# Turning the second FFN's gated tiles by VectorE in 32x32 blocks and by transfers between partition groups

## The chip, the core and the metric

The kernel runs on one core of a Trainium2 chip. TensorE multiplies matrices, VectorE and ScalarE do elementwise work, GpSimd issues the accumulating transfers and SyncE the plain ones; 16 DMA engines carry both. The metric is the device time of one execution in microseconds (us), the median of three runs, 2597.21.

## The reference, cut to what matters

One transformer-like layer: a half-step FFN, token mixing, a second half-step FFN, and a final norm. What the change touches is the second FFN:

```
def half_step_ffn(x, mod, i, g, w_up, w_down):
    h = adaln(x, g, mod, i)
    a, b = jnp.split(h @ w_up, 2, axis=-1)
    return x + 0.5 * mod[:, i + 2, None, :] * ((jax.nn.silu(a) * b) @ w_down)
```

Here x has 256 tokens of 2048 features, and the hidden width is 5632. The gated tensor silu(a) * b comes out with tokens on the partitions, and the product with w_down wants hidden rows on the partitions: each 128x128 piece must be turned.

## The kernel before

Every fp32 weight tile of 128x2048 (1 MB) comes from HBM, and `split` (L128, L129) makes of each half a rounded part `hi` (ScalarE) and a rest `lo` (VectorE); `mm3` (L152) makes three products of the parts. The pools hold four halves of hi and lo, three plain tiles `raw`, and two pairs of kept tiles, `chain` and `ra`.

The hidden width is cut into eleven blocks of 512. Block 0 and block 10 are computed directly. Blocks 1 to 9 go through `quad(n)`: a product of 2x2 sub-blocks in seven instead of eight products, over two token halves t = 0 and 1. Its seven steps run in the order a11, a12, n1, s4, s2, s3, a22, each over two weight tiles, q = 0 and 1, so over four halves; their results stand in the PSUM tiles X and Y. The tiles `ca` and `cy` gather them into the gated 128x512 tile of each token half: t = 0 is ready after s2 (`c12`), t = 1 after a22 (`c21`). The next block begins with a11.

The weights of a block are sums, made in part by accumulating transfers. SyncE issues: `again` (L2121), the two tiles with which the next block starts; `plain` (L2125), two raw tiles; the two plain loads in `first` (L2130); and `load_split` (L143), the down-projection's raw tiles. GpSimd issues the accumulating ones (`accum`, L731). chain and ra change roles from block to block. Beside the seven steps a unit of the down-projection, `down(n, n + 1)`, runs after four of them (after a12, n1, s2 and s3 of each block): one raw tile, and `mm <- hid2h, hid2l`.

`turned()` (L2041) turns a waiting gated tile N_TURN = 2 steps after it was made: four transposes on TensorE into PSUM (L2055), then the same two parts, hid2h by ScalarE (L2058, with the sign) and hid2l by VectorE (L2060). An order of steps is written by hand in `sequence`; the framework places each engine's instructions by its own plan, and every engine works through its list in order, so an instruction that waits holds all behind it. Each transfer signals on one of eight completion lanes for SyncE (DMAHW0 to 7), taken in turn, and eight for GpSimd (DMASW); a lane is taken again when its last transfer has landed.

## Time and profile before

| | |
|---|---|
| runs | 2602.92, 2593.06, 2597.21 us, median 2597.21 |
| profiled execution, its span | 2595.9 us |
| TensorE busy | 2570.6 us, 99% |
| VectorE, ScalarE, GpSimd busy | 2190.7, 1431.0, 220.6 us |
| granted TensorE clock, mean | 0.997 |
| moved from HBM | 664.59 MB read |
| second FFN's blocks 1 to 8 | about 2008 to 2492 us of the span, 60.6 us each |

How to read it: a row of a timeline has the start and the duration in us, the engine (SPq and POOLq are the issues of SyncE and GpSimd), the line, the operation, what is written and read, and how many. In brackets stands the idle time before and what ended it. In a row of groups, after the bar: busy us, the mean ns of one, then the idle time before. A row of waits has the total in us, how often, and the longest. A transfer's last figure is the time from issue to landing in us. Block 4's cycle begins near 2190 us.

### The profile page before, as it was taken

Reading aid. Unit: us, or ns where it says so; the run is one execution under the profiler, and the core shown is the slowest. Engines: PE = TensorE matmul, PEld = TensorE weight load, DVE = VectorE, ACT = ScalarE, POOL = GpSimd, SP = SyncE. Lnnn points to the kernel's source line nnn. Section 1 sums busy time; section 2 is a strip of 40 time slices with the busy share of each in tenths; the row PEclk is TensorE's granted clock in tenths of the full one; section 3 lists DMA queues with packets and bytes.
Section 4 is the critical chain, followed back from the end, with each engine's and each line's share of the span. In section 5 each row is a group of like instructions: output and inputs, shape, how many; then the busy total and the mean of one; then the engine's idle time right before and its main releaser. Section 6 shows DMA issues by size and latency. Waiting matters only on the chain. (4 is left out here: it accounts for less than half of the span.)

```text
span 2595.9 us, 34150 instructions
## 1 busy us (share of the span) xinstructions
PE 2570.6 (99%) x12646; PEld 2138.6 (82%) x12646; DVE 2190.7 (84%) x2884; ACT 1431.0 (55%) x1838; POOL 220.6 (8%) x271
## 2 busy tenths in 40 slices
PE   8999999999999999999999999999999999999998
PEld 5688888888888888888889989888898888888887
DVE  7788888878888788888887898798889888888887
ACT  5354444545444465444454448456486676666664
POOL 0000000100001100000110000120000000001001
PEclk9999999999999999999999999999999999999999
DMA  9889999999999989989986897776768999999985
GB/s 399 340 220 264 265 291 266 263 275 288 260 291 253 280 249 243 214 223 225 225 257 256 294 326 241 239 278 218 260 235 250 275 274 284 278 281 279 272 247 173
DMA packets 127655, 684.71 MB, mean 264 GB/s; under 512 B 14200, under 2 KB 16760, under 8 KB 64896
## 3 DMA queue, kind: packets, MB, share of 16 engines
q1 hardware_dynamic: 98112, 490.63, 50.4%
q0 software_dynamic: 29376, 191.90, 37.5%
q8 instruction: 99, 1.62, 0.2%
q14 instruction: 68, 0.56, 0.1%
HBM read 664.59 MB, written 17.89 MB: 263 GB/s over the span
## 5 line engine op out<-in xcount | busy, mean ns | idle before, releaser
L128 ACT ACTIVATE hi<-raw 128x1024 fp32r<-128x1024 f32 (+2 forms) x488 | 505.6, 1040 | 411.4 <-PE mm L152 314.0
L129 DVE TENSOR_TENSOR lo<-raw,hi 128x1024 fp32r<-128x1024 f32 (+2 forms) x476 | 569.3, 1204 | 137.9 <-ACT hi L128 117.7
L128 ACT ACTIVATE hi<-chain 128x1024 fp32r<-128x1024 f32 x352 | 372.0, 1060 | 305.0 <-PE mm L152 174.2
L129 DVE TENSOR_TENSOR lo<-chain,hi 128x1024 fp32r<-128x1024 f32 x352 | 426.5, 1221 | 106.9 <-ACT hi L128 98.1
L152 PE MATMUL mm<-hi,hhi 128*128 128x512 f32 (+3 forms) x1024 | 394.2, 385 | 0.0
L152 PE MATMUL mm<-lo,hhi 128*128 128x512 f32 (+3 forms) x1024 | 387.0, 378 | 0.2 <-DVE lo L129 0.2
L152 PE MATMUL mm<-hi,hlo 128*128 128x512 f32 (+3 forms) x1024 | 386.4, 377 | 0.0
L208 DVE SCALAR_TENSOR_TENSOR junk<-sraw,cBh 128x1024 fp8e5<-128x1024 f32 x192 | 234.4, 1221 | 22.8 <-DMA sraw<-in_w_mt 20.5
L152 PEld LDWEIGHTS mm<-lo,hhi 128*128 128x128 f32 x1024 | 192.5, 188 | 34.5 <-DVE lo L129 0.6
L152 PEld LDWEIGHTS mm<-hi,hhi 128*128 128x128 f32 x1024 | 192.6, 188 | 31.3 <-ACT hi L128 0.4
L152 PEld LDWEIGHTS mm<-hi,hlo 128*128 128x128 f32 x1024 | 192.8, 188 | 30.7
L129 DVE TENSOR_TENSOR lo<-ra,hi 128x1024 fp32r<-128x1024 f32 x104 | 126.3, 1222 | 27.2 <-ACT hi L128 23.1
L128 ACT ACTIVATE hi<-ra 128x1024 fp32r<-128x1024 f32 x104 | 110.1, 1061 | 67.6 <-PE mm L152 40.8
L152 PE MATMUL mm<-hi,hid2h 128*128 128x512 f32 x352 | 137.0, 389 | 0.0
L152 PE MATMUL mm<-lo,hid2h 128*128 128x512 f32 x352 | 137.0, 389 | 0.0
L152 PE MATMUL mm<-hi,hid2l 128*128 128x512 f32 x352 | 137.0, 389 | 0.0
L152 PE MATMUL mm<-hi,sumshl 128*128 128x512 f32 x400 | 123.1, 389 | 0.0
L731 POOL DMA_DIRECT2D chain<-in_w_up1b x60 | 53.0, 884 | 731.2 <-DVE lo L129 731.2
L208 DVE SCALAR_TENSOR_TENSOR sr<-sr,cBl 128x1024 f32<-128x1024 f32 x84 | 102.0, 1222 | 15.2 <-DMA sr<-in_w_mt 14.5
L152 PE MATMUL mm<-hi,sumshh 128*128 128x512 f32 x352 | 108.3, 389 | 0.0
L152 PE MATMUL mm<-hhi,hi 128*128 128x512 f32 (+1 forms) x288 | 101.4, 352 | 0.0
L152 PE MATMUL mm<-hhi,lo 128*128 128x512 f32 (+1 forms) x288 | 99.0, 344 | 0.0
(490 smaller groups left out, 5451.0 us busy)
## 6 DMA issues: line engine op xcount, KB each, us to landing
raw<-in_w_dn SPq DMA_DIRECT2D x70, 1024.0 KB, 9.3
chain<-in_w_up1b POOLq DMA_DIRECT2D x60, 1024.0 KB, 10.8
sraw<-in_w_mt SPq DMA_DIRECT2D x96, 512.0 KB, 8.4
sr<-in_w_mt SPq DMA_DIRECT2D x81, 512.0 KB, 5.4
raw<-in_w_up1b SPq DMA_DIRECT2D x40, 1024.0 KB, 8.0
mraw<-in_w_m SPq DMA_DIRECT2D x32, 1024.0 KB, 7.5
chain<-in_w_dn POOLq DMA_DIRECT2D x30, 1024.0 KB, 8.9
chain<-in_w_up2b POOLq DMA_DIRECT2D x28, 1024.0 KB, 11.1
```

What stands on the lines that cost most here:

```text
L128: scalar[0].activation(hi, src, AF.Copy)
L129: vector[0].tensor_tensor(lo, src, hi.bitcast(F32), op=ALU.subtract)
L152: tensor[0].matmul(out_ap, s, m, start=first and not n, stop=last and n == 2, skip_group_check=skip)
L208: ins = nc.vector.scalar_tensor_tensor(junk() if junk else raw, raw, 1.0, cB[s], op0=ALU.mult, op1=ALU.mult, accum_out=mT[:, i, s, kt, h : ...
L731: accum = lambda dst, src: nc.gpsimd.dma_start(dst, src, accum_op=ALU.add)
```

## The change

The gated tiles of blocks 1 to 8 no longer pass through TensorE. VectorE turns each 32x32 block of a 128x512 tile in place of its own (`nc.vector.transpose`, into the spare tile that held the other factor: ca for t = 0, cy for t = 1). A step later SyncE issues 16 transfers from SBUF to SBUF, each of 32 partitions x 128 elements (16 KB), which move partition group a of the spare tile to group b of a new tile x, of which there is one. Four steps after the turn hid2h and hid2l are made from x, with an output in runs of 32. The sign now goes into the gated product. The hidden rows stand in another order in a block, so the host lays out w_ffn2_down's rows for these blocks accordingly, in tiles of the same size. Block 9 and block 10 keep TensorE's transposes; N_TURN falls from 2 to 1.

```
-N_TURN = 2
+N_TURN = 1
+N_MOVE = 4
...
-            n, t, sa, sign = turn[0]
+            n, t, sa, spare = turn[0]
...
-            tb = tbank()
-            for j in range(FB):
-                nc.tensor.transpose(tb[:, j * P : (j + 1) * P], sa[:, j * P : (j + 1) * P], ident)
-            t3 = tb.rearrange("p (j c) -> p j c", j=FB)
             hh, hl = (x[:, :, t * P : (t + 1) * P] for x in hids[n])
-            nc.scalar.activation(hh, t3, AF.Copy, scale=sign)
-            if sign < 0:
-                nc.vector.scalar_tensor_tensor(hl, t3, -1.0, hh.bitcast(F32), op0=ALU.mult, op1=ALU.subtract)
-            else:
-                nc.vector.tensor_tensor(hl, t3, hh.bitcast(F32), op=ALU.subtract)
-            done.add((n, t))
+            if spare is None:
+                tb = tbank()
...
+                return
+            nc.vector.transpose(spare, sa)
+            x = f2b.tile([P, CB], F32, name="x", bufs=1)
+            by_runs = lambda y: y.rearrange("p j (a c) -> p a j c", c=32)
+            moved.append((clock[0], x, spare, n, t, by_runs(hh), by_runs(hl), x.rearrange("p (a j c) -> p a j c", a=4, j=FB)))
+
+        def parts_of(hh, hl, x):
+            nc.scalar.activation(hh, x, AF.Copy)
+            nc.vector.tensor_tensor(hl, x, hh.bitcast(F32), op=ALU.subtract)
+
+        def arrived():
+            for then, x, spare, n, t, *parts in list(moved):
+                if clock[0] == then + 1:
+                    for a in range(4):
+                        for b in range(4):
+                            dst, src = (slice(32 * i, 32 * i + 32) for i in (b, a))
+                            nc.sync.dma_start(x[dst, a * P : (a + 1) * P], spare[src, b * P : (b + 1) * P])
+                elif clock[0] == then + N_MOVE:
+                    parts_of(*parts)
+                    done.add((n, t))
+                    moved.pop(0)
...
-            mul = lambda o, x, y: nc.vector.tensor_tensor(o, x, y, op=ALU.mult)
+            negative = lambda o, y: nc.vector.scalar_tensor_tensor(o, o, -1.0, y, op0=ALU.mult, op1=ALU.mult)
...
-                mul(g["a"], g["a"], g["b"])
-                wait_turn(n, 0, g["a"], -1.0)
+                negative(g["a"], g["b"])
+                wait_turn(n, 0, g["a"], g["b"] if n != QUADS[-1] else None)
...
-                mul(g["a"], g["a"], g["y"])
-                wait_turn(n, 1, g["a"], -1.0)
+                negative(g["a"], g["y"])
+                wait_turn(n, 1, g["a"], g["y"] if n != QUADS[-1] else None)
```

The order on SyncE in block 4, before: the two raw tiles of `plain`, the two chain tiles of `again`, a down-projection tile, the two ra tiles of `first`, three down-projection tiles.

```order
L2125 DMA raw<-in_w_up2b 128x2048 x2
L2121 DMA chain_16106<-in_w_up2b 128x2048
L2121 DMA chain_16107<-in_w_up2b 128x2048
L143 DMA raw<-in_w_dn 128x2048
L2130 DMA ra_16108<-in_w_up2b 128x2048
L2130 DMA ra_16109<-in_w_up2b 128x2048
L143 DMA raw<-in_w_dn 128x2048 x3
```

The same stretch of SyncE's list now:

```order
L2149 DMA raw<-in_w_up2b 128x2048 x2
L2145 DMA chain_16106<-in_w_up2b 128x2048
L2083 DMA x<-ca 32x128 x16
L2145 DMA chain_16107<-in_w_up2b 128x2048
L2154 DMA ra_16108<-in_w_up2b 128x2048
L2154 DMA ra_16109<-in_w_up2b 128x2048
L145 DMA raw<-in_w_dn 128x2048
L2083 DMA x<-cy 32x128 x16
L145 DMA raw<-in_w_dn 128x2048 x3
```

All 16 pieces of t = 0 stand between the two chain tiles, the first down-projection tile has moved behind the ra tiles, and t = 1's 16 pieces stand behind it. Blocks 1, 2, 6 and 8 have t = 0's pieces in this place too; in 3, 5 and 7 four of them stand ahead of the second tile of `again`, and twelve behind it.

The same place with SyncE's waits, from the first chain tile to the ninth piece (a transfer's own lane is the first DMAHW that it waits for, where there is one; the first piece also waits for VectorE's turn):

```order
L2145 DMA chain_16106<-in_w_up2b 128x2048 [waits DMAHW6_49,DMASW2_49,DVE_49]
L2083 DMA x<-ca 32x128 [waits DMAHW1_49,DMAHW7_49,DMAHW0_49,DVE_49]
L2083 DMA x<-ca 32x128 x3
L2083 DMA x<-ca 32x128 [waits DMAHW3_49]
L2083 DMA x<-ca 32x128 [waits DMAHW4_49]
L2083 DMA x<-ca 32x128 [waits DMAHW5_49]
L2083 DMA x<-ca 32x128 [waits DMAHW6_49]
L2083 DMA x<-ca 32x128 [waits DMAHW7_49]
```

The first chain tile is on lane 6, the pieces take lanes 7, 0, 1, 2 and so on, and the eighth waits for lane 6, which is that chain tile's landing.

On ScalarE, around the last tile of a22 in block 4, before (L2105 is the copy of X in `c22`, L2109 the silu in `c21`):

```order
L2058 ACTIVATE hid2h<-tr 128x4x128
L128 ACTIVATE hi<-raw 128x1024 x2
L128 ACTIVATE hi<-ra_16108 128x1024 x2
L2105 ACTIVATE ca<-X 128x512
L128 ACTIVATE hi<-ra_16109 128x1024 x2
L128 ACTIVATE hi<-chain_16106 128x1024 x2
```

And now:

```order
L2129 ACTIVATE ca<-X 128x512
L130 ACTIVATE hi<-ra_16109 128x1024
L2071 ACTIVATE hid2h<-x 128x4x4x32
L130 ACTIVATE hi<-ra_16109 128x1024
L130 ACTIVATE hi<-chain_16106 128x1024 x2
```

The hid2h copy of t = 0 has moved from ahead of the down-projection's halves to between the two halves of a22's last tile, and it waits for all eight lanes on which its pieces land.

More of the change, by code (lines that the diff above doesn't have):

```diff
@@ L2052, in turned, with wait_turn @@
             turn.pop(0)
-            tb = tbank()
-            for j in range(FB):
-                nc.tensor.transpose(tb[:, j * P : (j + 1) * P], sa[:, j * P : (j + 1) * P], ident)
-            t3 = tb.rearrange("p (j c) -> p j c", j=FB)
             hh, hl = (x[:, :, t * P : (t + 1) * P] for x in hids[n])
-            nc.scalar.activation(hh, t3, AF.Copy, scale=sign)
-            if sign < 0:
-                nc.vector.scalar_tensor_tensor(hl, t3, -1.0, hh.bitcast(F32), op0=ALU.mult, op1=ALU.subtract)
-            else:
-                nc.vector.tensor_tensor(hl, t3, hh.bitcast(F32), op=ALU.subtract)
-            done.add((n, t))
+            if spare is None:
+                tb = tbank()
+                for j in range(FB):
+                    nc.tensor.transpose(tb[:, j * P : (j + 1) * P], sa[:, j * P : (j + 1) * P], ident)
+                x = tb.rearrange("p (j c) -> p j c", j=FB)
+                parts_of(hh, hl, x)
+                done.add((n, t))
[7 more added lines that the diff above has]
+            nc.vector.tensor_tensor(hl, x, hh.bitcast(F32), op=ALU.subtract)
+        moved = []
+        def arrived():
[7 more added lines that the diff above has]
+                    parts_of(*parts)
+                    done.add((n, t))
+                    moved.pop(0)
         done = set()
-        def wait_turn(n, t, sa, sign):
-            turn.append((n, t, sa, sign))
+        def wait_turn(n, t, sa, spare):
+            turn.append((n, t, sa, spare))
             born[n, t] = clock[0]
@@ L2193, in up @@
                                 nc.vector.tensor_tensor(sab[t], sab[t], bs[t], op=ALU.mult)
-                                wait_turn(n, t, sab[t], 1.0)
+                                wait_turn(n, t, sab[t], None)
                             else:
@@ L2265, in tile_layer @@
             clock[0] += 1
+            arrived()
             turned()
@@ L2268, in tile_layer @@
             assert next(x, x) is x
-        while turn:
+        while turn or moved:
             clock[0] += 1
+            arrived()
             turned()
@@ L2376, in _laid_out @@
     m["w_mt"] = asc(wm[:, 2:].reshape(D, 7, KT, P).transpose(1, 2, 3, 0))
+    runs = lambda dn: dn.reshape(NF // FB, 4, FB, 32, NCB, CB).transpose(0, 4, 1, 3, 2, 5).reshape(NF // FB, NCB, P, 2048)
     for n in "12":
@@ L2391, in _laid_out @@
         m[f"w_pre{n}"] = asc(np.concatenate(loads))
-        m[f"w_dn{n}"] = asc(dn.reshape(NF // FB, FB, P, NCB, CB).transpose(0, 3, 2, 1, 4).reshape(NF // FB, NCB, P, 2048))
+        rows = dn.reshape(NF // FB, FB, P, NCB, CB).transpose(0, 3, 2, 1, 4).reshape(NF // FB, NCB, P, 2048)
+        if n == "2":
+            rows = np.concatenate([rows[:1], runs(dn)[1:-2], rows[-2:]])
+        m[f"w_dn{n}"] = asc(rows)
     w = a["w_in"][0]
```

## The prediction

> **What bounds the kernel now.** I read the page first, then the table of stretches for the second FFN, SyncE's waits, SyncE's issues of one block, and last TensorE, ScalarE and the transfers around those issues.

> ```profile
> span 2595.9 us, 34150 instructions
> PE 2570.6 (99%) x12646; PEld 2138.6 (82%) x12646; DVE 2190.7 (84%) x2884; ACT 1431.0 (55%) x1838; POOL 220.6 (8%) x271
> 2189.40:2250.00 60.60, 60.20 (x270) 49.39 (x269) 53.52 (x52) 41.06 (x44) 4.91 (x6) 1.00 0.93 273
> ```

> The first two rows are the page's: TensorE is busy for 99% of the span. The third is one stretch of 60.6 us, the length of one block of the second FFN, with the busy time of PE, PEld, DVE, ACT and POOL, the granted clock, the DMA engines' share and GB/s. TensorE lacks 0.4 us there, VectorE works 53.5 us, and the 16 DMA engines are taken for 93%. So TensorE sets the end, and DMA comes close behind it. What is in reserve shows in stretches of 2 us inside this block:

> ```profile
> 2204.00:2206.00 2.00, 2.00 (x10) 1.68 (x9) 1.31 (x2) 0.13 (x1) 0.00 (x0) 1.00 1.02 422
> 2210.00:2212.00 2.00, 2.00 (x11) 1.65 (x10) 2.00 (x3) 1.61 (x2) 0.00 (x0) 1.00 1.03 434
> 2232.00:2234.00 2.00, 2.00 (x11) 1.64 (x9) 1.97 (x3) 2.00 (x4) 0.00 (x0) 1.00 0.46 193
> 2234.00:2236.00 2.00, 1.59 (x7) 1.03 (x6) 2.00 (x3) 1.07 (x2) 0.00 (x0) 1.00 0.02 8
> 2236.00:2238.00 2.00, 2.00 (x10) 1.62 (x10) 2.00 (x2) 1.34 (x2) 0.00 (x0) 1.00 0.04 4
> ```

> The DMA share is 1.0 except for about 5 us, 2233 to 2238. That is the whole reserve of a block, and it comes late in the cycle. Next, what SyncE's queue waits for in the same block, and its issues:

> ```profile
> SPq L2125 <- DVE lo L129: 21.5, 2, 14.7
> SPq L143 <- DVE lo L129: 15.2, 4, 7.9
> 2190.22 0.33 SPq L2125 DMA_DIRECT2D raw<-in_w_up2b  x1
> 2193.31 5.39 SPq L2121 DMA_DIRECT2D chain<-in_w_up2b  x2
> 2201.56 0.33 SPq L143 DMA_DIRECT2D raw<-in_w_dn  x1
> 2204.66 5.82 SPq L2130 DMA_DIRECT2D ra<-in_w_up2b  x2
> 2218.41 5.76 SPq L143 DMA_DIRECT2D raw<-in_w_dn  x3
> ```

> SyncE waits most of the time for VectorE to leave a weight buffer, and issues a load the moment it may. The loads are just in time, so whatever holds this queue delays them. I call the two chain loads G1 (2193.3) and G2 (it ends with the row, so 2198.4), the ra loads R1 and R2, the first down-projection load D1 (2201.6). Their landings (KB, us from issue to landing: G1, G2, then D2 at 2218.4, then the raw load at 2237.0, alone on the engines):

> ```profile
> chain<-in_w_up2b SPq DMA_DIRECT2D x1, 1024.0 KB, 13.5
> chain<-in_w_up2b SPq DMA_DIRECT2D x1, 1024.0 KB, 10.9
> raw<-in_w_dn SPq DMA_DIRECT2D x1, 1024.0 KB, 11.8
> raw<-in_w_up2b SPq DMA_DIRECT2D x1, 1024.0 KB, 4.7
> ```

> **What is taken from TensorE.** 16 tiles with four transposes each leave; blocks 9 and 10 keep theirs. One group in block 4:

> ```profile
> 2195.83 0.40 PE L152 MATMUL mm<-lo,hid2h 128*128 128x512 f32 x1
> 2196.07 0.60 PE L2055 MATMUL tr<-ident,ca 128*128 128x128 f32 x4
> 2196.43 0.71 PE L152 MATMUL X<-hi,s3f 128*128 128x512 f32 x2
> 2196.97 0.39 PE L152 MATMUL X<-lo,s3f 128*128 128x512 f32 x1
> ...
> 2197.65 0.39 PE L152 MATMUL X<-lo,s3f 128*128 128x512 f32 x1
> ```

> From one lo product to the next is 0.68 us in steady state (2196.97 to 2197.65), and 1.14 across the group (2195.83 to 2196.97): 0.46 us a group, and 16 x 0.46 = 7.4 us on the path. This is all that the change can give, beside the 0.4 us a block that TensorE idles.

> **The arithmetic around it** moves little:

> ```profile
> L2078 DVE TENSOR_TENSOR ca<-ca 128x512 f32<-128x512 f32 x9 | 6.2, 685 | 0.0
> L2060 DVE SCALAR_TENSOR_TENSOR hid2l<-tr,hid2h 128x512 fp32r<-128x512 f32 x16 | 10.9, 683 | 0.0
> L2077 DVE TENSOR_TENSOR chain<-chain,ra 128x1024 f32<-128x1024 f32 x16 | 19.2, 1220 | 0.1
> L2058 ACT ACTIVATE hid2h<-tr 128x512 fp32r<-128x512 f32 x16 | 9.4, 588 | 0.7 <-PE tr L2055 0.4
> ```

> The gated product becomes a scalar_tensor_tensor and the lo part a tensor_tensor: 683 against 685 ns, nothing. ScalarE's copy keeps 588 ns; source and strides differ, for which I take 0 between -0.1 and +0.2 us a tile, off the path. VectorE gains one 32x32 turn of 128x512: no row shows one, so between 0.69 us (a pass of that size) and 1.22 (twice the elements), and I take 0.7. That is 1.4 us a block on an engine with 7 us free; its cover is that idle time, and if it fails up to 2.4 us a block show.

> **SyncE's queue and the transfers.** This is where I expect the price. Each tile adds 16 transfers of 16 KB, 256 in all, on the queue that feeds the weights. Nearest rows for price and pace: a transfer of exactly 32 rows of 512 bytes (how long it took, then its issue and the next one's), a 256 KB one at the program's end, and a queue that has eight transfers out:

> ```profile
> cc<-in_cc SPq DMA_DIRECT2D x1, 16.0 KB, 1.6
> 0.80 0.40 SPq L190 DMA_DIRECT2D cc<-in_cc  x1
> 1.25 0.41 SPq L601 DMA_DIRECT2D vecs<-in_vecs  x1
> out<-acc SPq DMA_DIRECT2D x1, 256.0 KB, 2.3
> 7.16 0.33 SPq L421 DMA_DIRECT2D raw<-in_w_pre  x1
> SPq L421 <- DMA mraw<-in_w_m: 1.3, 1, 1.3
> ```

> One lands after 1.6 (16 KB) to 2.3 us (256 KB); I take 2.0. An issue costs 0.33 us alone; back to back, 0.80 to 1.25, it is 0.45, whatever the size. I take 0.45; the ends are 0 and 0.6. The last two rows are the ninth transfer of the program, held until the third had landed: SyncE uses eight completion lanes in turn and waits for the lane. The built program has these waits on the new transfers (quoted with the change): in block 4 G1 holds lane 6 and x's eighth piece needs lane 6. So piece 8 cannot go before G1 has landed, and G2, R1, R2, D1 stand behind all 16.

> Of DMA time the pieces are small: 256 KB a tile at the 422 to 434 GB/s above are 0.6 us, and at half that pace 1.2, so 1.2 to 2.4 us a block against a reserve of 5.

> Block 4, step by step. G1 lands at 2193.3 + 13.5 = 2206.8. Piece 8 goes then, pieces 9 to 16 follow at 0.45, the last at 2210.4, landed at 2212.4. G2 goes at 2210.9 and not at 2198.4: the engines, full till G1's end, stand nearly empty for some 5 us.

> Who waits for x? ScalarE: its hid2h copy now stands between two weight copies, and whatever follows waits behind it.

> ```profile
> 2206.06 1.06 ACT L128 ACTIVATE hi<-ra 128x1024 fp32r<-128x1024 f32 x1 [1.93 <-PE mm L152]
> 2207.43 1.06 ACT L128 ACTIVATE hi<-ra 128x1024 fp32r<-128x1024 f32 x1 [0.31 <-PE mm L152]
> 2220.19 1.05 ACT L128 ACTIVATE hi<-raw 128x1024 fp32r<-128x1024 f32 x1
> 2211.48 0.39 PE L152 MATMUL Y<-hi,h2hi 128*128 128x512 f32 x1
> 2224.24 0.39 PE L152 MATMUL mm<-hi,hid2h 128*128 128x512 f32 x1
> ```

> It stands between the first two rows. ScalarE resumes at 2212.4: 0.59 for hid2h, 1.06 for hi, then 1.22 on VectorE for lo, 2215.3. TensorE wants this half at 2211.48 (fourth row: fourth half of the product that begins at 2207.40), less the 0.46 saved: 2211.0. It waits 4.3 us.

> R2 waits for that lo: 2215.4; D1 behind it: 2215.8, 14 us late. Alone it would land 4.7 later and be in time. But the next two accumulating loads are on the engines then, as they were for D2, so I take D2's 11.8: 2227.6, and 2229.9 as hi and lo. TensorE wants it at 2224.24 (fifth row; the third is ScalarE's copy of it), less 0.92 saved, plus 4.3: 2227.6. Another 2.3 us. Together 6.6 us.

> The second tile of a block (cy) queues behind D1 and ahead of D2, D3 and D4. D2's use moves with the 6.6 us, D3 and D4 are wanted far later: nothing, at most 2 us.

> Blocks 1, 2, 6 and 8 have the same order. In 3, 5 and 7 G2 goes after four pieces, in time, but a later piece needs its lane: G2 lands at 2198.4 + 10.9 = 2209.3, the last piece goes at 2211.1, lands at 2213.1. The hid2h copy stands one half into the next product, so the half is ready at 2213.1 + 2.9 = 2216.0, wanted at 2207.40 + 5 x 1.36 (the 2211.48 of the fourth half gives 4.08 for three) - 0.46 = 2213.7: 2.3 us. D1 goes at 2212.4, is ready at 2226.5, wanted at 2225.6: 0.9. Together 3.2.

> Sum: 5 x 6.6 + 3 x 3.2 - 7.4 = 35.2 us. The profiled span of 2595.9 becomes 2631; it lies 1.3 us under the median of 2597.2 of the three runs, so I say **2632 us**. Low end: issues that cost nothing and 1.6 us landings leave 1.9 and 0.1 us, and D1 in time: 9.8 - 7.4 = +2.4, 2600. High end: D1 with G1's 13.5 adds 1.7 us to each block, and 2 us for the second tile: +30, 2662.

> [...]

> **Rivals.** (a) The queue has room and the transfers hide: 2597 - 7, 2590, no change that can be measured. For it: D1 is issued 18.6 us ahead of its copy. Against: G1's 13.5 us are in the trace and the lane makes the queue wait them out. It decides if pieces land by 2208.1: then the half is ready at 2211.0. (b) TensorE's clock drops at the new stalls. The trace knows half clock early on:

> ```profile
> 18.00:28.00 10.00, 9.91 (x57) 5.75 (x59) 7.87 (x19) 8.42 (x16) 1.18 (x2) 0.50 1.02 424
> ```

> Ten us at 0.50, after a start with idle gaps, cost 5 us. One such time in each of the five longer-stalled blocks, plus 25: 2657. For it: 4.3 us without work. Against: no gap in this stage is that long, so nothing shows it. [...] (c) The waits land elsewhere: the second tile holds ScalarE as well, another 3 us a block, 2656. (d) It is faster by more than 0.5%, 13 us: more than the 7.4 + 8 x 0.4 that TensorE can give; only an error of mine.

> **Chances.** Forecast, 2610 to 2650: 0.58. (a), with everything down to a few us of loss: 0.22. (b) and (c): 0.17. (d): 0.03. Half a per cent, 13 us, is about what a measurement of this kernel tells from no change; so slower 0.75, same 0.22, faster 0.03. The range 2600 to 2665 leaves out about 0.12 below and 0.05 above.

> **What the profile after would show.** SyncE's waits gain a large group on x, put down to G1's and G2's landings; G2 goes 10 us later after VectorE's release in five blocks; ScalarE shows idle before hid2h<-x, some 3 to 6 us a tile for ca; TensorE's idle in the blocks rises from 0.4 us to 3 to 7, before a22's last half and before the first down-projection of each block; DMA's share shows a second hole after G1. If the issues of x take no longer than before and ScalarE never idles there, the prediction is wrong, and 2590 is right. If TensorE idles but before n1 or s4, the place is wrong.

## The result, and the profile after

The changed kernel takes 2698.4 us (median of four runs, 2695.64 to 2699.29) against 2598.84: the ratio is 1.0389, 95% interval 1.0377 to 1.0401. The direction was forecast, the size was not: +100 us instead of +35.

The page's first rows after, the span and the busy time of each engine:

```profile
span 2697.6 us, 34416 instructions
PE 2605.2 (97%) x12582; PEld 2149.6 (80%) x12582; DVE 2200.4 (82%) x2900; ACT 1426.5 (53%) x1838; POOL 220.4 (8%) x271
```

TensorE has 64 matmuls less to do and is busy for 34.6 us more (2605.2 against 2570.6). The rest of its span, where it is not busy, has grown from 25.3 to 92.4 us, by 67.1. The two make 101.7 us, the difference of the two profiled spans. So there are two separate losses: TensorE waits, and TensorE runs slower. First the waits, TensorE's in the second FFN (total, how often, longest):

```profile
PE Y L154 <- ACT hi L130: 28.8, 9, 5.3
PE mm L154 <- ACT hi L130: 20.0, 6, 10.2
PE X L154 <- ACT hi L130: 7.9, 3, 3.0
PE mm L154 <- DVE lo L131: 6.0, 8, 2.0
PE Y L154 <- DVE lo L131: 4.7, 8, 1.0
```

It never waits for hid2h; but for 0.2 us it waits for the two parts of a weight half. Y is mostly a22's product, X the next block's a11, mm the down-projection. Who keeps ScalarE, in the same stretch:

```profile
ACT hid2h L2071 <- DMA x<-ca: 49.8, 8, 7.6
ACT hi L130 <- DMA raw<-in_w_dn: 34.9, 12, 6.2
ACT hid2h L2071 <- DMA x<-cy: 25.0, 8, 9.5
```

Two things: its in-order wait for x, for both tiles of a block, and weights that land late. And SyncE's queue on the new transfers:

```profile
SPq L2083 <- DVE cy L2064: 42.2, 6, 7.8
SPq L2083 <- DMA x<-cy: 31.3, 27, 1.8
SPq L2083 <- DMA raw<-in_w_up2b: 29.6, 8, 4.4
SPq L2083 <- DMA raw<-in_w_dn: 21.4, 5, 6.5
SPq L2083 <- DMA ra<-in_w_up2b: 19.8, 4, 6.6
SPq L2083 <- DMA chain<-in_w_up2b: 15.4, 4, 4.3
```

The last four rows, 86 us, are the lane waits: a piece stands until a 1 MB load has landed. The first is the queue standing at a piece whose tile VectorE has not yet turned.

The chain in block 4, as a timeline of SyncE's issues:

```profile
2235.20 0.33 SPq L2145 DMA_DIRECT2D chain<-in_w_up2b  x1
2236.54 18.54 SPq L2083 DMA_DIRECT2D x<-ca  x16
2255.19 0.52 SPq L2145 DMA_DIRECT2D chain<-in_w_up2b  x1
...
2259.67 0.42 SPq L145 DMA_DIRECT2D raw<-in_w_dn  x1
```

And the timeline of ScalarE's copy from x and of TensorE around it (in brackets the idle time before):

```profile
2256.43 0.63 ACT L2071 ACTIVATE hid2h<-x 128x512 fp32r<-128x512 f32 x1 [6.41 <-DMA x<-ca]
...
2252.68 0.39 PE L154 MATMUL Y<-lo,h2hi 128*128 128x512 f32 x1
2258.06 0.79 PE L154 MATMUL Y<-hi,h2hi 128*128 128x512 f32 x1 [4.99 <-ACT hi L130]
2258.65 0.63 PE L154 MATMUL Y<-hi,h2lo 128*128 128x512 f32 x1
...
2275.78 0.50 PE L154 MATMUL mm<-hi,hid2h 128*128 128x512 f32 x1 [2.37 <-ACT hi L130]
```

G1 goes at 2235.2; the 16 pieces hold the queue for 18.5 us; G2 goes 20 us behind G1. ScalarE stands 6.4 us at x, TensorE 5.0 us at a22's last half and 2.4 us at the first down-projection. The forecast was 17.6 us for G2's lag and 4.3 and 2.3 us for TensorE's two stalls. What it left out stands in the fourth row: a product that took 0.39 us ahead of the stall takes 0.63 behind it. The same place as stretches (PE's busy time first, the granted clock third from the end):

```profile
2258.00:2263.60 5.60, 5.50 (x12) 3.91 (x13) 5.57 (x6) 3.94 (x6) 0.87 (x1) 0.50 0.98 407
2263.60:2270.40 6.80, 6.80 (x31) 5.59 (x31) 6.02 (x7) 5.17 (x6) 0.87 (x1) 1.00 1.02 292
```

Half clock for 5.6 us of work behind a stall of 5: 12 matmuls where the next 6.8 us have 31. The clock record of the trace has 15 such stretches between 2024 and 2571 us, 81.9 us in all; before there was none in this stage.

### The profile page after: what moved, and what is told of

It reads as the page before. It is cut to its first block, busy times and chain, and to the rows that moved or that the text cites. A ratio compares the mean times of both kernels' runs of the same rounds, so it can differ in the third digit from the quotient of the medians.

```text
span 2697.6 us, 34416 instructions
## 1 busy us (share of the span) xinstructions
PE 2605.2 (97%) x12582; PEld 2149.6 (80%) x12582; DVE 2200.4 (82%) x2900; ACT 1426.5 (53%) x1838; POOL 220.4 (8%) x271
## 3 DMA queue, kind: packets, MB, share of 16 engines
q8 instruction: 99, 1.62, 0.2%
## 4 chain that ended last, share of the span: by engine, by line
PE 28%; DMA 11%; DVE 5%; SPq 3%; issue 2%; ACT 2%; ACTq 0%; POOL 0%; POOLq 0%; DVEq 0%
PE mm L154 18%; DMA x<-cy 4%; PE Y L154 3%; SPq L2083 3%; PE X L154 2%; DMA ra<-in_w_up2b 2%; DVE lo L131 2%; DMA chain<-in_w_up2b 2%; DMA raw<-in_w_dn 1%; ACT hi L130 1%; DMA sr<-in_w_mt 1%; DMA x<-ca 1%; PE mm L1707 1%; PE tr L154 0%; PE tr L1527 0%
## 5 line engine op out<-in xcount | busy, mean ns | idle before, releaser
L131 DVE TENSOR_TENSOR lo<-chain,hi 128x1024 fp32r<-128x1024 f32 x352 | 425.6, 1220 | 106.0 <-ACT hi L130 100.5
L210 DVE SCALAR_TENSOR_TENSOR junk<-sraw,cBh 128x1024 fp8e5<-128x1024 f32 x192 | 234.2, 1220 | 21.5 <-DMA sraw<-in_w_mt 19.1
L154 PE MATMUL mm<-hi,hid2h 128*128 128x512 f32 x352 | 143.4, 407 | 20.0 <-ACT hi L130 20.0
L131 DVE TENSOR_TENSOR lo<-ra,hi 128x1024 fp32r<-128x1024 f32 x104 | 126.1, 1221 | 31.5 <-ACT hi L130 28.4
## 6 DMA issues: line engine op xcount, KB each, us to landing
raw<-in_w_dn SPq DMA_DIRECT2D x70, 1024.0 KB, 6.8
chain<-in_w_up1b POOLq DMA_DIRECT2D x60, 1024.0 KB, 9.8
raw<-in_w_up1b SPq DMA_DIRECT2D x40, 1024.0 KB, 8.3
mraw<-in_w_m SPq DMA_DIRECT2D x32, 1024.0 KB, 7.4
chain<-in_w_dn POOLq DMA_DIRECT2D x30, 1024.0 KB, 8.3
chain<-in_w_up2b POOLq DMA_DIRECT2D x28, 1024.0 KB, 13.1
```

What stands on the lines that cost most here:

```text
L131: vector[0].tensor_tensor(lo, src, hi.bitcast(F32), op=ALU.subtract)
L154: tensor[0].matmul(out_ap, s, m, start=first and not n, stop=last and n == 2, skip_group_check=skip)
L210: ins = nc.vector.scalar_tensor_tensor(junk() if junk else raw, raw, 1.0, cB[s], op0=ALU.mult, op1=ALU.mult, accum_out=mT[:, i, s, kt, h : ...
```

## The experiments

The theory after the result, Q: the pieces hold SyncE's queue, so weights land late (its half L), and ScalarE waits for x in order (its half S); TensorE's clock falls at the stalls. Its rivals: the time the pieces take on the DMA engines (D), and the new arithmetic (V). One table for all runs; a ratio is to runs of the kernel before that were made beside it, whose medians lie between 2594.73 and 2599.69 us; the two last columns are each profile's "not busy" (span less TensorE's busy time) and busy time, less those of the kernel before (25.3 and 2570.6 us).

| run | median, us | ratio to before, 95% interval | not busy, us | busy, us |
|---|---|---|---|---|
| the changed kernel | 2698.4 | 1.0389 (1.0377 to 1.0401) | +67.1 | +34.6 |
| no transfers | 2593.98 | 0.9984 (0.9975 to 0.9994) | +4.7 | -4.3 |
| transfers beside the kernel before | 2722.33 | 1.0478 (1.0463 to 1.0494) | +90.7 | +31.1 |
| 4 pieces of 64 KB | 2667.3 | 1.0268 (1.0252 to 1.0284) | +44.9 | +28.3 |
| ScalarE issues | 2819.36 | 1.0853 (1.0832 to 1.0873) | +188.7 | +35.1 |
| hid2h later | 2723.0 | 1.0493 (1.0477 to 1.0509) | +98.5 | +28.5 |
| GpSimd issues | 2733.64 | 1.0531 (1.0514 to 1.0548) | +93.6 | +36.0 |
| GpSimd issues, hid2h later | 2633.71 | 1.0150 (1.0133 to 1.0167) | +25.2 | +10.7 |
| stalls of known length (two runs) | 2651.38 | 1.0216 (1.0196 to 1.0237) | +35.4 | +18.2 |
| only t = 0 moved | 2677.5 | 1.0301 (1.0286 to 1.0316) | +53.6 | +26.8 |
| only t = 1 moved | 2638.42 | 1.0149 (1.0130 to 1.0167) | +27.7 | +11.6 |
| 4 pieces, hid2h later | 2604.13 | 1.0028 (1.0014 to 1.0042) | +4.8 | +0.2 |
| GpSimd issues, hid2h later still | 2625.4 | 1.0100 (1.0084 to 1.0115) | +24.0 | +2.5 |

### No transfers

```
-            x = f2b.tile([P, CB], F32, name="x", bufs=1)
+            x = spare
...
-                    for a in range(4):
-                        ...
-                            nc.sync.dma_start(x[dst, a * P : (a + 1) * P], spare[src, b * P : (b + 1) * P])
+                    pass
```

> Left out: the 256 transfers; hid2h and hid2l are made directly from the tile that VectorE turned in 32x32 blocks (its partition groups are not exchanged, so the gated values stand in other places than the reference has them). Everything else is the changed kernel. Theory Q (SyncE's queue: the pieces delay the weight loads and hold ScalarE, and TensorE's clock falls in the stalls): 2590 us, the kernel before less the 7.4 us of transposes; TensorE idles no more than 1 us a block and shows full clock. Theory V (VectorE's turn and the strided hid2h and hid2l cost the time): above 2640. Theory D (the DMA engines' time goes to the pieces): 2590 too.

2593.98 us. The whole loss is gone, so V falls: VectorE's turns and the strided parts cost nothing that shows. It also bounds the idea: with exchanges that cost nothing it would gain 0.06 to 0.25%, less than the 7.4 us that I had taken from TensorE. TensorE's busy time falls by 4.3 us only. TensorE's longest kind of wait in the second FFN is now this:

```profile
PE mm L154 <- DVE lo L131: 2.4, 7, 0.4
```

### The transfers alone, beside the kernel before

```
             done.add((n, t))
+            if n in QUADS[:-1]:
+                x = f2b.tile([P, CB], F32, name="x", bufs=1)
+                for a in range(4):
+                    for b in range(4):
+                        dst, src = (slice(32 * i, 32 * i + 32) for i in (b, a))
+                        nc.sync.dma_start(x[dst, a * P : (a + 1) * P], sa[src, b * P : (b + 1) * P])
```

> The kernel before, TensorE's transposes and all, and beside them the same 256 transfers of 16 KB on SyncE's queue, from the gated tile into a tile that nobody reads. So the queue is loaded as in the changed kernel and ScalarE waits for no piece. Theory Q with both halves (late weight loads, and ScalarE held by x): a part of the loss stays, 2630 to 2670, with TensorE waiting for weights of G2 and the down-projection and none at a22's last half; stalls shorter, and fewer stretches at half clock. If late loads alone do it: 2700, the changed kernel's time and the 7 us of transposes. If ScalarE's wait on x alone does it: under 2610. Theory D: 2700.

2722 us, above every number that I gave. Transfers that nobody reads cost more than the whole change. The waits of TensorE, ScalarE and SyncE in the second FFN of this kernel:

```profile
PE mm L152 <- ACT hi L128: 51.9, 7, 11.2
...
ACT hi L128 <- DMA raw<-in_w_dn: 84.5, 12, 14.2
ACT hi L128 <- DMA chain<-in_w_up2b: 38.9, 5, 12.3
...
SPq L2069 <- DVE ca L2084: 50.4, 15, 12.3
```

ScalarE now waits for the weights themselves: L alone is enough. The last row is the queue standing at the pieces until VectorE has made the gated tile. That S costs nothing does not follow, since the two waits can stand in for each other; the later runs tell.

### Four pieces of 64 KB in place of sixteen

```
                     for a in range(4):
-                        for b in range(4):
-                            dst, src = (slice(32 * i, 32 * i + 32) for i in (b, a))
-                            nc.sync.dma_start(x[dst, a * P : (a + 1) * P], spare[src, b * P : (b + 1) * P])
+                        nc.sync.dma_start(x[32 * (3 - a) : 32 * (4 - a)], spare[32 * a : 32 * a + 32])
```

> The changed kernel with 4 transfers of 32 partitions x 512 (64 KB) in place of 16 of 32 x 128 (16 KB) for each tile: the same bytes, a quarter of the issues. Left out: the exchange within a partition group's columns, so the values are not the reference's. Theory Q: the queue is taken for 4 x 0.63 = 2.5 us instead of 10 and few lanes are waited for; the pieces still stand behind G1 (14 us) on the engines, so ScalarE still waits some us for t = 0: 2600 to 2640. Theory D (bytes count): 2698, no change against the changed kernel.

2667 us, 27 above my range for Q, 31 below D. The bytes are the same, so D falls as the whole cause as far as it goes by bytes. The joined pieces also have runs of 2 KB instead of 512 bytes; that these do not make most of the loss is shown by the runs further down in which GpSimd issues the same 16 KB pieces (2634 and 2625 us). The queue is free after 2.8 us, and TensorE has no long wait for a down-projection any more. The timeline of the issues in block 4, and the waits:

```profile
2222.20 2.81 SPq L2081 DMA_DIRECT2D x<-ca  x4
```

```profile
PE Y L154 <- ACT hi L130: 32.4, 15, 3.7
...
ACT hid2h L2071 <- DMA x<-ca: 58.9, 8, 8.1
ACT hid2h L2071 <- DMA x<-cy: 42.9, 8, 6.3
```

What is left is S: the pieces are issued at once but land 8 to 15 us later, among the 1 MB loads, and ScalarE stands at them, for both tiles of a block.

### ScalarE issues the pieces

```
-                            nc.sync.dma_start(x[dst, ...
+                            nc.scalar.dma_start(x[dst, ...
```

> The changed kernel with the 256 pieces issued by ScalarE instead of SyncE. Theory Q: SyncE's loads go when they went before the change; pieces have lanes of their own and no 1 MB load ahead of them in their queue, and land in 2 to 3 us. But ScalarE issues for 16 x 0.6 = 10 us a tile, and no weight half is rounded in that time: TensorE has 4 halves' cover of 1.36 us each and stalls some 3 to 5 us a tile, 16 tiles: 50 to 80 us and the clock beside it, 2640 to 2690. If issues by ScalarE cost it little, under 2600. Theory D: 2698.

2819 us, the slowest of all. "Lanes of their own" was wrong. One tile's issues in the timeline, then waits of ScalarE and SyncE:

```profile
2317.60 16.06 ACTq L2083 DMA_DIRECT2D x<-cy  x16
```

```profile
ACT hi L130 <- DMA x<-ca: 118.2, 8, 21.6
...
SPq L2145 <- DMA x<-ca: 78.8, 5, 16.3
```

The last row is the loads of `again` on SyncE, which wait 78.8 us for pieces that ScalarE issued; the down-projection loads wait 59.0 us for them. A load and a piece have no tile in common: what these loads wait for is a completion lane. (In the changed kernel's trace SyncE's 932 transfers signal on eight semaphores in turn, GpSimd's 204 on eight others.) So SyncE's queue is not freed, and ScalarE rounds no weights for 16 us a tile.

### hid2h later, on SyncE's queue

```
-N_MOVE = 4
+N_MOVE = 7
...
-            nc.scalar.activation(hh, x, AF.Copy)
+            tc.keep_in_program_order(nc.scalar.activation(hh, x, AF.Copy))
```

> The changed kernel with hid2h made 7 steps after the turn instead of 4, and kept in that place of ScalarE's list; SyncE's list is as in the changed kernel. So the queue delays the weights as before, but ScalarE meets x two to six halves later. Theory L (late weight loads alone make the loss): 2680 to 2700, TensorE's waits for hi stay, now put down to the weights' landings instead of x. Theory S (ScalarE held by x): the first tile's stall at a22 goes, some 4 to 5 us a block with the clock, 2640 to 2655.

2723 us: not the 2640 to 2655 of S, 23 above the range of L, and 25 us worse than the changed kernel. There is one tile x; read later, it holds the next tile's pieces, and the queue with them. Waits of SyncE and ScalarE:

```profile
SPq L2083 <- DVE hid2l L2072: 49.2, 3, 16.8
...
ACT hi L130 <- DMA raw<-in_w_dn: 97.3, 11, 14.9
ACT hid2h L2071 <- DMA x<-ca: 17.7, 5, 4.3
```

ScalarE's wait for t = 0's x has fallen from 49.8 to 17.7 us, and its wait for down-projection weights has risen from 34.9 to 97.3. With the queue held, freeing ScalarE gains nothing.

### GpSimd issues the pieces, with hid2h at its place and later

The first edit is `nc.gpsimd.dma_start` in the place of `nc.sync.dma_start`; the second adds the two edits just shown.

> The changed kernel with the 256 pieces issued by GpSimd, which signals on lanes of its own. Theory L: SyncE's loads go as before the change, so no down-projection or chain tile is late by the queue; GpSimd spends 16 x 0.9 = 14 us a tile on the issues, which pushes accumulating loads behind them back by up to that, and ScalarE still waits for x, at the same place, until 14 us and a landing after the turn. 2620 to 2680, with TensorE's stalls at a22's last half. If the DMA engines' time for 16 KB pieces is the cause (theory D): 2698.

> Both edits: pieces issued by GpSimd, and hid2h made 7 steps after the turn in a kept place of ScalarE's list. Theory L and S together: neither SyncE's loads nor ScalarE wait any longer; what is left is accumulating loads that start up to 14 us later behind the pieces: 2595 to 2625, most of the loss gone. If some other cost of the transfers is at work (their time on the DMA engines): above 2650.

2733.64 and 2633.71 us. In the first TensorE waits at a22 for t = 0 and at the next block's n1 for t = 1, never for a down-projection, and ScalarE at x for both tiles; in the second most of that is gone, though it is 9 us above my 2595 to 2625. The waits of the first and then of the second:

```profile
PE Y L154 <- ACT hi L130: 95.7, 16, 8.0
...
ACT hid2h L2071 <- DMA x<-ca: 89.7, 8, 12.3
ACT hid2h L2071 <- DMA x<-cy: 51.8, 8, 7.6
```

```profile
PE X L154 <- ACT hi L130: 14.5, 5, 3.6
...
ACT hid2h L2071 <- DMA x<-ca: 31.1, 5, 6.6
```

With SyncE's queue left as it was, the later hid2h saves 100 us; with the queue held it lost 25. My 2620 to 2680 for the first was too low: S alone is worth as much as the whole loss when x is 16 issues of GpSimd and a landing away.

### Four pieces, and hid2h later

> Four transfers of 64 KB a tile on SyncE's queue, as in the run with joined pieces (the exchange of columns is left out as there), and hid2h made 7 steps after the turn in a kept place. If two waits, each enough by itself, make the loss (SyncE's queue taken up by issues and lanes; ScalarE in order behind x): both are now short, 2595 to 2620, 50 us less than with joined pieces alone, though the same edit made the 16-piece kernel 25 us slower. If the transfers cost by their bytes or their place behind G1: 2650 or more.

2604.13 us, as expected, 0.28% above the kernel before. This closes the square:

| | hid2h after 4 steps | after 7 steps, in a kept place |
|---|---|---|
| 16 pieces on SyncE | 2698.4 | 2723.0 |
| 4 pieces on SyncE | 2667.3 | 2604.1 |
| 16 pieces on GpSimd | 2733.6 | 2633.7 |

Each of the two waits is enough for most of the loss. Either alone taken away leaves 2667 or more; both taken away, it is 2604 with four pieces and 2634 from GpSimd, where ScalarE still stands at x for t = 0, for 31 us.

### One tile of the two

For t = 0 alone `wait_turn(n, 1, g["a"], None)`, for t = 1 alone `wait_turn(n, 0, g["a"], None)`.

> The changed kernel with only the first tile of each block (t = 0, from ca) moved by transfers; t = 1 goes through TensorE. Its hidden rows then stand in the other order than w_ffn2_down's, so half of the values are not the reference's. By the prediction's sum nearly the whole loss belongs to this tile (the wait at a22 and the late D1): 2690. If the two tiles share it by their waits for x in the trace (49.8 and 25.0 us of ScalarE): 2655 to 2670.

> The changed kernel with only the second tile (t = 1, from ca into cy) moved by transfers; t = 0 goes through TensorE, with the same reservation on the values. By the prediction's sum (nothing, at most 2 us a block): 2595 to 2610. If the second tile's pieces hold the down-projection loads behind them, as SyncE's 42 us of waits for VectorE's turn of cy suggest: 2630 to 2650, with TensorE waiting ahead of the down-projections' first halves (mm).

2677.5 and 2638.42 us, +78 and +39 against 2599.36: the first between the two numbers expected, the second within the higher range. The second tile is far from free. The waits of TensorE and ScalarE with t = 1 alone:

```profile
PE mm L154 <- DVE lo L131: 22.9, 8, 3.3
...
ACT hid2h L2071 <- DMA x<-cy: 36.1, 8, 6.8
```

And VectorE's row in block 4 of that run, on its timeline:

```profile
2252.29 0.69 DVE L2072 TENSOR_TENSOR hid2l<-x,hid2h 128x512 fp32r<-128x512 f32 x1 [3.13 <-ACT hid2h L2071]
```

Eight waits of TensorE, of up to 3.3 us, at the lo part of a down-projection tile: ScalarE stands at x for t = 1, VectorE at hid2l behind it, and the lo part stands behind hid2l. The mechanism that I expected, down-projection loads held in the queue, is not what these rows show.

### Stalls of known length

Blocks 1 to 8 get 7 to 17 copies that nobody reads, ahead of a22's third half on ScalarE; `keep_in_program_order` holds them and a22's hi copies in their places.

```
+LADDER = 7, 8, 9, 10, 11, 12, 14, 17
...
+                    kept_order[0] = m == 6 and n != QUADS[-1]
+                    if kept_order[0] and q:
+                        junk = f2b.tile([P, CB], F32, name="junk", bufs=1)
+                        for _ in range(LADDER[i]):
+                            tc.keep_in_program_order(nc.scalar.activation(junk, h2hi[:, :2, :T].bitcast(F32), AF.Copy))
```

> The kernel before, and in blocks 1 to 8 7, 8, 9, 10, 11, 12, 14 and 17 copies of 128x512 (0.59 us each) that nobody reads, on ScalarE ahead of a22's last two halves, nothing else. ScalarE has about 3.7 us to spare there, so TensorE should stand still for about 0.4, 1.0, 1.6, 2.2, 2.8, 3.4, 4.5 and 6.3 us, 22 us in all. Theory C3 (the clock halves only behind a stall of more than 3.4 us): half clock in two or three of the blocks, 2625. Theory C1 (stalls of 1.7 to 3 us are enough where they fall badly): half clock in five or six blocks, with 1.7 to 3.4 us lost each: 2632 to 2640. If stalls cost nothing but their length: 2619 and full clock.

2651.38 us: the copies took 0.63 us, and TensorE stood for 35.4 us instead of 22; on top its busy time rose by 18.2. Block 2's place in the timeline of TensorE, with one of its two stalls, and then stretches of 3.4 us there, in block 3 and in block 6 (PE's busy time first, the clock third from the end):

```profile
2086.73 0.50 PE L158 MATMUL Y<-hi,h2hi 128*128 128x512 f32 x1 [1.63 <-ACT hi L132]
```

```profile
2084.90:2088.30 3.40, 1.24 (x4) 0.59 (x4) 1.59 (x2) 3.14 (x5) 0.00 (x0) 1.00 0.68 289
2088.30:2091.70 3.40, 3.40 (x9) 2.64 (x8) 0.77 (x1) 3.24 (x6) 0.00 (x0) 0.50 0.44 130
...
2153.20:2156.60 3.40, 1.72 (x10) 1.27 (x9) 0.93 (x2) 2.30 (x4) 0.00 (x0) 1.00 1.01 429
2156.60:2160.00 3.40, 2.87 (x12) 1.88 (x11) 2.13 (x2) 3.27 (x6) 0.00 (x0) 1.00 0.38 118
...
2361.40:2364.80 3.40, 1.53 (x7) 0.86 (x6) 0.44 (x1) 3.31 (x5) 0.00 (x0) 1.00 1.01 419
2364.80:2368.20 3.40, 3.04 (x8) 2.08 (x7) 3.40 (x4) 3.25 (x4) 0.00 (x0) 0.50 0.30 58
```

C3 falls: blocks 2 and 6 had no stall above 1.9 us and went to half clock all the same. C1 holds, with half clock in six blocks, though its 2632 to 2640 us were too low for 35 us of stalls. Behind the stall in block 2 comes a wait of 0.5 us for lo, so the stretch holds 1.24 us of work, and the next one runs at half clock. So it is behind 1.53 us of work (the last two rows), and not behind 1.72 (the two rows between). Ten stalls of 1.6 to 7.2 us stand in this run; two of 1.6 and one of 1.9 brought a stretch of 3.4 us at half clock, one of 1.7 and two of 1.6 did not, the four of 3.9 to 7.2 brought 6.8 to 10.2 us. In the changed kernel's clock record the 15 stretches at half clock last 3.41, 6.83 or 10.24 us and begin whole multiples of 3.41 us apart. On this grid its stage (1990 to 2580 us) has 13 stretches at full clock with less than 1.5 us of TensorE's work, and half clock followed all 13; it followed two of the three with 1.5 to 1.8 us, and none of the 132 with more. The kernel before has more than 1.8 us of work in all its 172, and no half clock there. Over the fourteen traces the counts are 108 of 108, 6 of 15 and none of 2062.

### hid2h later still, pieces from GpSimd

`N_MOVE = 8, 7`, one more step for t = 0.

> GpSimd issues the pieces, and hid2h is made 8 steps after the turn for t = 0 and 7 for t = 1, in a kept place: one step more for t = 0 than in the run before. There TensorE's five stalls of 3.3 to 5.5 us came from ScalarE at x of t = 0, 6 us too early at most, about the length of one step: they should go, and the half clock with them: 2600 to 2615. If x's landing is not what it waits for but the accumulating loads behind the pieces: still 2630.

2625.4 us, 8 less than before that step, 10 above what I expected. The half clock is nearly gone (busy +2.5 instead of +10.7), TensorE's waits are not (+24.0 instead of +25.2): they are now short and spread, and ScalarE's cy copy stands behind x instead. TensorE's longest group of waits:

```profile
PE Y L154 <- ACT cy L2115: 8.6, 3, 4.6
```

No version that made the exchange came below the kernel before, and the run without transfers says that 6.5 us would be the most to win.

## Why the prediction was wrong, step by step

**TensorE's saving** (7.4 us): the busy time fell by 4.3 us without transfers, not by 7.4, and the median time by 5.7. The price of a group was read rightly: in the trace of the kernel before, the 15 groups without a wait of their own cost 0.45 to 0.49 us each. Why not all of it shows is open; TensorE's time not busy is 4.7 us longer in that run, with short new waits for lo.

**The arithmetic** (nothing): right. VectorE's turn took what I chose, 0.71 us (chosen: 0.7); hid2h from x took 0.04 us more than from PSUM, off the path. Groups by line of the changed kernel:

```profile
L2064 DVE STREAM_TRANSPOSE ca<-ca 128x512 f32<-128x512 f32 x8 | 5.7, 713 | 0.3
...
L2071 ACT ACTIVATE hid2h<-x 128x512 fp32r<-128x512 f32 x16 | 10.1, 630 | 74.8 <-DMA x<-ca 49.8 <-DMA x<-cy 25.0
```

**SyncE's queue for t = 0**: right in kind and nearly in size. The eighth piece did wait for G1's landing (it went at 2249.5, 14.3 us behind G1); a lone piece in block 4 landed 1.7 to 1.8 us after its issue (taken: 2.0); one followed another at 0.63 us, above my upper end of 0.6. The least that a piece took here was 1.7 us from SyncE and 1.6 from GpSimd. Each block has the stall where the prediction put it: 5.31, 4.07, 4.99, 4.69 and 4.23 us at a22's last half in blocks 1, 2, 4, 6 and 8 (forecast 4.3), 3.01, 2.21 and 2.72 in the next block's a11 in 3, 5 and 7 (forecast 2.3), 31.2 us together against 28.4. Four issues a tile instead of sixteen gained 31 us (2667.3 against 2698.4) and left 68: joined, the pieces still landed 8 to 15 us late.

**The rest of a block's waits** (D1 2.3 and 0.9 us, the second tile "nothing, at most 2 us"): here the first step failed. 67.1 less 31.2 leaves 36 us against a forecast of 14.2 (4.7 of the 36 stand in the run without transfers too). Block 1 has one stall of 10.2 us: there ScalarE stands 9.5 us at x for t = 1, and all four down-projection tiles stand behind that tile's 16 pieces, so the first lands another 3.5 us later. I said that block 1 has block 4's order, and SyncE's issues show otherwise. That block 4's first down-projection stalls 2.4 us, against 2.3, is luck: its load took 14.9 us to land instead of 11.8, but half clock brought TensorE there later too, 15.4 us behind the first stall's end where the kernel before takes 12.8. And I let the second tile hold loads only. It holds ScalarE as t = 0 does: 25.0 us of waits for x<-cy, and by itself it costs 39 us. That was rival (c); its 3 us a block is what t = 1 alone shows (27.7 us not busy over eight blocks, 3.5 each).

**The clock** is the larger failure: rivals (b) and (c), which I gave 0.17 together, both came true. TensorE's busy time is 34.6 + 4.3 = 39 us above that of the run without transfers. In the 15 stretches at half clock TensorE works for 67.6 us, with 0.43 us from one product to the next instead of 0.23; by these figures half clock cost some 32 us, an estimate, and the other 7 are not accounted for. The sum had nothing for it. I argued that no gap in this stage was long enough to show it, and priced five times 5 us. In fact the 15 stretches followed eleven of the twelve stalls above 2 us, and four stretches of 3.4 us in which shorter stalls of 1.1 to 2.0 us stand. I had counted the five stalls of 4.3 us alone. But half clock followed all 13 stretches of 3.41 us with less than 1.5 us of work and none of the 132 with more than 1.8, and in the run with stalls of known length it followed two stalls of 1.6 us and one of 1.9.

**The sum**: waits 67.1 instead of 42.6, half clock some 32 instead of nothing, and TensorE's saving, which shows as 4.3 of 7.4. The first two errors go the same way and are one family: a stall was priced by its own length, at one place, for one tile.

**What the profile was to show**: SyncE's and ScalarE's groups on x, G2 late, TensorE idle at a22 and the first down-projection came as written. The DMA engines were not filled up: their share in the stretch from 2250.0 to 2310.6 us, as long as the one shown before, is 0.81, where it was 0.93.

What stays open: how the queue's loss divides between the issues, the lanes and the waits for VectorE's turn was not measured apart; SyncE's rows give 86 us for the lanes, 42 for the turn and 31 for the pieces' own landings, but only the part counts that delays a load which is needed.

## What to carry to other kernels

Before work is moved off a busy engine by many small transfers, write out what stands behind them in the queue that issues them and what stands behind their reader in its engine's list: these are two separate waits, each can cost most of it, and taking away one alone can show little or even a loss. Price every new stall of TensorE with the clock as well: in the changed kernel about 0.5 us of half-clock loss came with each us of waiting (32 with 67), also in stalls of 2 to 3 us. And ask first what the removed work was worth: here at most 6.5 us in 2597, against a loss of 100 with sixteen issues a tile.
